# adaLN chunks of a two-layer diffusion backbone beside the first FFN: result columns on the tile's rows, products on GpSimd, row sums on ScalarE

## The chip, the cores and the metric

The kernel runs on one core of a Trainium2 chip. The metric is the device time of one execution in microseconds. A core has five engines that run side by side, each in its own program order: TensorE (PE; its weight loads are PEld), VectorE (DVE), ScalarE (ACT), GpSimd (POOL) and SyncE (SP), which here issues all DMAs. An engine waits at an instruction until the semaphores that it names are reached, and everything behind it on that engine waits too.

## What is computed

A batch of one: 512 latent tokens and 256 context tokens of width 1024 pass through two layers. Layer 0 mixes by windowed attention, layer 1 by a gated short convolution. Every layer takes six vectors of 1024 from the conditioning vector c (adaLN), which shift, scale and gate its two halves.

```
def adaln(cvec, w, b):
    m = (jax.nn.silu(cvec) @ w + b)[..., None, :]
    return jnp.split(m, 6, axis=-1)

for i in range(DEPTH):
    sh1, sc1, g1, sh2, sc2, g2 = adaln(c, ada_w[i], ada_b[i])
    ...
    h = h + g1 * y_lat
    h = h + g2 * conv_ffn(modulate(rms_norm(h, norm_ffn[i]), sh2, sc2), ffn_w_up[i], ffn_conv[i], ffn_w_down[i])

def conv_ffn(a, w_up, conv_w, w_down):
    g, u = jnp.split(dwconv3(a @ w_up, conv_w), 2, axis=-1)
    return (jax.nn.silu(g) * u) @ w_down
```

The hidden width of the FFN is 2816. A chunk of adaLN is one product of the vector silu(c) with a 1024x1024 matrix. All arrays are fp32.

## The kernel before

**Tiling.** Activations lie transposed: eight tiles of 128 channels by 512 tokens (`h`). A weight piece is a tile of 128x1024 that is loaded (`wraw`, four buffers), split by ScalarE into a high half (`whi`, a cast) and by VectorE into a low half (`wlo`, a subtraction), seven pieces in a ring (L177). Each product of a piece with an activation takes three matmuls, high by high, high by low and low by high (`mm3`, L195).

**FFN.** `ffn` (L808) goes through the hidden width in three thirds of 8, 8 and 6 tiles. For each hidden tile j two pieces of the up projection run over all eight channel tiles (48 matmuls of 512 columns); ScalarE and VectorE then evaluate the three taps of the convolution, silu and the product, and split the hidden tile into `g` tiles, high (ScalarE, L164) and low (VectorE, L165). After a third, `out_proj` (L759) runs its down projection, eight pieces, each over all hidden tiles of the third. The first four pieces of the first third run in two halves of 256 tokens, and the norm ahead of it is made in two halves as well (`norm_half`, L754): TensorE sums the squares over channels, ScalarE and VectorE take the root (`rcol`), TensorE spreads it over rows, and VectorE and ScalarE modulate eight tiles into `a`.

**adaLN.** The chunks that attention and the first norm need are made earlier. Seven chunks of 1024 results (the gate of the first FFN, and six for layer 1) are made beside the first FFN. `tail0` (L841) is called after each hidden tile with two steps and after each piece of the down projection with one. A step (`ada_step`, L239) takes 128 of the 1024 inputs: two loads of 128x512 into `araw` (four buffers); GpSimd multiplies each half by the column of silu(c) that belongs to its rows (L261) and adds it to an accumulator `adaacc` (L263). After eight steps, `ada_cols` (L277) turns the two accumulators with eight transposes on TensorE, VectorE sums each 128 columns (L274) and adds the bias (L275). The first of these GpSimd instructions waits for the end of the norm's second half (`add_manual_dep`, L253).

**Order.** In the attention an order written out by hand holds; from the FFN on, a scheduler orders each engine's instructions by its own estimate of when each can run, and that order is fixed in the program. Chip times do not change it.

Of the kernel before, what the change touches and what calls it, by code (L numbers as in the profile page):

```python
# [94 lines left out]
def kernel(ctx: ExitStack, tc: tile.TileContext, xT, ctxT, par_d, rope_d, mask_d, ident_d,  # L95
                         ada0_d, ada_d, wqkv_d, wo_d, wup_d, wdown_d, wsc_d, wsco_d, out_d):
    nc = tc.nc
    vec, act, pool, pe, sp = nc.vector, nc.scalar, nc.gpsimd, nc.tensor, nc.sync
# [8 lines left out]
    def nm(s):  # L107
        uid[0] += 1
        return f"{s}{uid[0]}"
# [15 lines left out]
    def nbank():  # L125
        t = ring[ringpos[0] % 8]
        ringpos[0] += 1
        return bank(t)
# [12 lines left out]
    ident = cp.tile([P, P], F32, name="ident")  # L141
# [94 lines left out]

    adastate = {}

    def ada_step(layer, ch, kt):  # L239

        raws = []
        for half in range(2):
            w = adastate["raw"]()
            sp.dma_start(out=w, in_=ada_d[layer, ch, kt, :, half * 512:(half + 1) * 512])
            raws.append(w)
        if kt == 0:
            adastate["acc"] = [adastate["acc_alloc"]() for _ in range(2)]
        acc = adastate["acc"]
        for half in range(2):
            ins = ada_mult_add(acc[half], raws[half], kt)  # L250
            after = adastate.pop("after", None)
            if after is not None:
                tc.add_manual_dep(ins.ins, after.ins.name, DEP, reason="the norm has VectorE's port for itself")  # L253
        if kt == KT - 1:
            adadone.append((layer, ch, acc))

    adadone = []

    def ada_mult_add(a, w, kt):
        c_ = cs[:, kt, 0:1]  # L260
        ins = pool.tensor_scalar(out=w if kt else a, in0=w, scalar1=c_, scalar2=1.0, op0=ALU.mult, op1=ALU.mult)  # L261
        if kt:
            pool.tensor_tensor(out=a, in0=a, in1=w, op=ALU.add)  # L263
        return ins

    def ada_transpose(acc, ps=None):
        ps = bank("qt") if ps is None else ps
        for i in range(4):
            pe.transpose(out=ps[:, i * P:(i + 1) * P], in_=acc[:, i * P:(i + 1) * P], identity=ident)
        return ps  # L270

    def ada_columns(layer, ch, half, ps):
        col = ada[layer][:, ch, half * 4:half * 4 + 4]
        vec.tensor_reduce(out=col, in_=ps.rearrange("p (a b) -> p a b", a=4), axis=AX.X, op=ALU.add)  # L274
        vec.tensor_tensor(out=col, in0=col, in1=pc("adab", (layer * 6 + ch) * KT + half * 4, 4), op=ALU.add)  # L275

    def ada_cols():  # L277

        layer, ch, acc = adadone.pop(0)
        banks = [ada_transpose(acc[half], nbank()) for half in range(2)]  # L280
        for half in range(2):
            ada_columns(layer, ch, half, banks[half])
# [11 lines left out]
    with ExitStack() as attn:  # L294
# [22 lines left out]
        with tc.tile_pool(name="start", bufs=1, reuse_waits="tile") as st:  # L317
# [10 lines left out]
            accs = {}  # L328
# [345 lines left out]
        def ad(i):  # L674
            for hf in range(2):
                tmps["a", i, hf] = w = ap.tile([P, 512], F32, tag="araw", name=nm("araw"), bufs=4)
                sp.dma_start(out=w, in_=ada_d[0, 2 + i // 8, i % 8, :, hf * 512:(hf + 1) * 512])

# [7 lines left out]
        def AT(ch, hf):  # L686
            tmps["A", ch, hf] = ada_transpose(accs[ch, hf])

        def AR(ch, hf):
            ada_columns(0, 2 + ch, hf, tmps["A", ch, hf])  # L690

# [11 lines left out]
    with tc.tile_pool(name="ffn", bufs=1, reuse_waits="tile") as fp, four_banks() as sp3:  # L703
# [3 lines left out]

        adastate["raw"] = lambda: fp.tile([P, 512], F32, tag="araw", name=nm("araw"), bufs=4)
        adastate["acc_alloc"] = lambda: fp.tile([P, 512], F32, tag="aacc", name=nm("adaacc"), bufs=4)

# [40 lines left out]
        def norm_begin(slot, shift):  # L751
            return {"acc": f(), "slot": slot, "shift": shift, "ah": [at() for _ in range(KT)], "al": [at() for _ in range(KT)]}
# [43 lines left out]
        lead_tail = [wpiece(None, 1024, raw) for raw in lead_raw]  # L796
        splits[:] = (3, 6)

        def last_cols():
            banks = [ada_transpose(accs[2, hf], nbank()) for hf in range(2)]  # L800
            for hf in range(2):
                ada_columns(0, 4, hf, banks[hf])
# [34 lines left out]

        late = [0, 0]
        fsteps = [(0, 5, kt) for kt in range(KT)] + [(1, ch, kt) for ch in (1, 0, 4, 3, 2, 5) for kt in range(KT)]
# [12 lines left out]

        def after_ffn0():
            assert not fsteps
            while adadone:
                ada_cols()
# [11 lines left out]
        first = proj([wpiece(wsc_d[i]) for i in (KT, 2 * KT, KT + 1, 2 * KT + 1)], ah, al, True, 4, second)  # L868
# [84 lines left out]
```

## Time and profile before

| what | us |
|---|---|
| median of three runs (lowest, highest) | 1238.05 (1236.66, 1239.66) |
| the profiled execution | 1238.28 |
| its span in the profile | 1236.5 |
| TensorE busy in the span | 1198.2 |
| VectorE, ScalarE, GpSimd busy | 733.0, 478.1, 401.7 |

The profile lists every instruction of one execution. A group row gives line, engine, operation, output and inputs with shapes and count; then the busy time in us and the mean of one in ns; then the idle time of the engine ahead of these instructions and what ended it. A timeline row gives the start and the duration in us, then the same names; in square brackets stands the idle time ahead of it. A row of waits names who waited, for whom, for how long in all, how often, and the longest. The time of an instruction includes what it loses once it has begun, for instance at a shared port. The first FFN runs on TensorE from about 290 to 688 us.

### The profile page before, as it was taken

The numbers are of one execution on the slowest core, as the hardware profiler recorded it, in microseconds if no ns is written. First come the engines' busy times: TensorE is split into PE (matmuls) and PEld (weight loads), VectorE is DVE, ScalarE is ACT, GpSimd is POOL, SyncE is SP. The second block draws the span as 40 slices with busy tenths as digits, with TensorE's granted clock in tenths as the row PEclk, the third lists the DMA queues.
The fourth block names the chain that finished last, engine by engine and source line by source line (L and its number), as shares of the span: only waits on it lengthen the run. The fifth ranks groups of instructions, "written<-read, shape, count | busy, mean of one in ns | idle before, by whom it ended". The sixth has DMA issues, their size and how long they took to land.

```text
span 1236.5 us, 16557 instructions
## 1 busy us (share of the span) xinstructions
PE 1198.2 (97%) x6414; PEld 980.2 (79%) x6414; DVE 733.0 (59%) x1128; ACT 478.1 (39%) x785; POOL 401.7 (32%) x358
## 2 busy tenths in 40 slices
PE   8999999999995999989999999999999999999998
PEld 6676666689883788878888988889988888888888
DVE  4688788647667545764665664444675446643652
ACT  4434777625334123322333442233454233432430
POOL 0059688510995893979601000001000000000000
PEclk8999999999997999999999999999999999999999
DMA  9445143252366455465423243332143233333211
GB/s 363 162 151 169 60 154 113 72 179 74 120 229 213 157 192 177 154 221 180 161 69 102 69 136 103 91 97 85 36 153 102 89 100 103 89 99 91 76 39 68
DMA packets 58382, 157.61 MB, mean 127 GB/s; under 512 B 6592, under 2 KB 8640, under 8 KB 58304
## 3 DMA queue, kind: packets, MB, share of 16 engines
q1 hardware_dynamic: 58304, 156.56, 38.6%
q8 instruction: 50, 0.82, 0.3%
q14 instruction: 28, 0.23, 0.1%
HBM read 152.86 MB, written 2.10 MB: 125 GB/s over the span
## 4 chain that ended last, share of the span: by engine, by line
PE 74%; POOL 12%; DVE 5%; issue 4%; DMA 2%; ACT 2%; SPq 0%; POOLq 0%; ACTq 0%; DVEq 0%
PE ps_s L198 10%; PE ps_s L196 10%; PE ps_s L197 10%; POOL adaacc L263 6%; PE ps_pt L196 5%; PE ps_pt L197 5%; PE ps_pt L198 5%; POOL araw L261 4%; PE ps_oa L660 3%; PE ps_pt L641 3%; PE ps_qt L197 2%; PE ps_qt L198 2%; PE ps_s L580 2%; PE ps_qt L196 2%; PE ps_oa L196 2%
## 5 line engine op out<-in xcount | busy, mean ns | idle before, releaser
L165 DVE TENSOR_TENSOR wlo<-wraw,whi 128x1024 fp32r<-128x1024 f32 (+2 forms) x194 | 228.0, 1183 | 183.9 <-ACT whi L164 179.0
L164 ACT CAST whi<-wraw 128x1024 fp32r<-128x1024 f32 (+2 forms) x194 | 183.3, 953 | 358.1 <-PE ps_s L197 153.0
L263 POOL TENSOR_TENSOR adaacc<-adaacc,araw 128x512 f32<-128x512 f32 x126 | 181.4, 1447 | 7.0
L196 PE MATMUL ps_s<-a,whi 128*128 128x512 f32 (+1 forms) x480 | 180.2, 375 | 0.0
L197 PE MATMUL ps_s<-a,whi 128*128 128x512 f32 (+1 forms) x480 | 180.1, 375 | 0.0
L198 PE MATMUL ps_s<-a,wlo 128*128 128x512 f32 (+1 forms) x480 | 179.9, 375 | 0.0
L261 POOL TENSOR_SCALAR araw<-araw,cs 128x512 f32<-128x512 f32 x140 | 128.1, 918 | 39.0 <-DMA araw<-in_ada 39.0
L196 PE MATMUL ps_s<-g,whi 128*128 128x512 f32 (+1 forms) x304 | 105.2, 346 | 17.3 <-ACT g L164 17.3
L197 PE MATMUL ps_s<-g,whi 128*128 128x512 f32 (+1 forms) x304 | 104.6, 345 | 0.0
L198 PE MATMUL ps_s<-g,wlo 128*128 128x512 f32 (+1 forms) x304 | 104.4, 344 | 0.0
L196 PEld LDWEIGHTS ps_s<-a,whi 128*128 128x128 f32 x480 | 90.4, 188 | 16.2
L198 PEld LDWEIGHTS ps_s<-a,wlo 128*128 128x128 f32 x480 | 90.4, 188 | 16.2
L197 PEld LDWEIGHTS ps_s<-a,whi 128*128 128x128 f32 x480 | 90.4, 188 | 16.1
L198 PE MATMUL ps_pt<-a,wlo 128*128 128x512 f32 (+1 forms) x256 | 92.9, 363 | 0.0
L196 PE MATMUL ps_pt<-a,whi 128*128 128x512 f32 (+1 forms) x256 | 92.9, 363 | 0.0
L197 PE MATMUL ps_pt<-a,whi 128*128 128x512 f32 (+1 forms) x256 | 92.8, 362 | 0.0
L749 DVE SCALAR_TENSOR_TENSOR h<-ps_s,ada,h 128x512 f32<-128x512 f32 (+1 forms) x45 | 28.3, 631 | 88.0 <-PE ps_s L198 87.9
L164 ACT CAST g<-f 128x512 fp32r<-128x512 f32 x52 | 32.3, 621 | 123.2 <-DVE f L826 122.6
L196 PEld LDWEIGHTS ps_s<-g,whi 128*128 128x128 f32 x304 | 57.7, 190 | 25.8 <-ACT g L164 18.4
L207 POOL TENSOR_TENSOR f<-f,t 128x512 f32<-128x512 f32 x6 | 9.5, 1582 | 205.0 <-ACT t L206 205.0
L197 PEld LDWEIGHTS ps_s<-g,whi 128*128 128x128 f32 x304 | 57.7, 190 | 8.2 <-DVE g L165 0.8
L198 PEld LDWEIGHTS ps_s<-g,wlo 128*128 128x128 f32 x304 | 57.8, 190 | 7.1
(297 smaller groups left out, 2518.6 us busy)
## 6 DMA issues: line engine op xcount, KB each, us to landing
wraw<-in_wup SPq DMA_DIRECT2D x88, 512.0 KB, 3.6
araw<-in_ada SPq DMA_DIRECT2D x160, 256.0 KB, 2.7
wraw<-in_wdown SPq DMA_DIRECT2D x32, 512.0 KB, 3.7
wraw<-in_wsc SPq DMA_DIRECT2D x24, 512.0 KB, 3.5
gw<-in_ada SPq DMA_DIRECT2D x16, 512.0 KB, 10.0
wraw<-in_wqkv SPq DMA_DIRECT2D x12, 512.0 KB, 7.1
wraw<-in_wdown SPq DMA_DIRECT2D x16, 384.0 KB, 3.1
wraw<-in_wo SPq DMA_DIRECT2D x8, 512.0 KB, 5.2
```

The source lines that it names most:

```text
L164: act.copy(out=hi, in_=raw)
L165: vec.tensor_tensor(out=lo, in0=raw, in1=hi.bitcast(F32), op=ALU.subtract)
L196: pe.matmul(out=ps, lhsT=wh, rhs=ah, start=start, stop=False)
L197: pe.matmul(out=ps, lhsT=wh, rhs=al, start=False, stop=False)
L198: pe.matmul(out=ps, lhsT=wl, rhs=ah, start=False, stop=stop)
L207: eng.tensor_tensor(out=acc, in0=acc, in1=sq[:, :n], op=ALU.add)
L261: ins = pool.tensor_scalar(out=w if kt else a, in0=w, scalar1=c_, scalar2=1.0, op0=ALU.mult, op1=ALU.mult)
L263: pool.tensor_tensor(out=a, in0=a, in1=w, op=ALU.add)
L580: pe.matmul(out=s[t][:, i, :w], lhsT=q2s[p][x][HALF[t], cl], rhs=KEYS[p // 4][(p // 2 + t) % 2][y][HALF[t], ks_], start=(n == 0), stop=(n ...
L641: pe.transpose(out=pt[:, q:q + P], in_=es[p, b, t][0][:, o:o + P], identity=ident)
L660: pe.matmul(out=r["po"][HALF[t], b0:b0 + n], lhsT=V[:, j, p // 2, :], rhs=pf[:, t * n:(t + 1) * n], start=first, stop=not r["left"])
L749: vec.scalar_tensor_tensor(out=h[m][:, cl], in0=ps[:, cl], scalar=gate[:, m:m + 1], in1=h[m][:, cl], op0=ALU.mult, op1=ALU.add)
```

## The change

The same seven chunks are made from another layout. The host stores these weights transposed (`adat`), so that a tile of 128x1024 has 128 result columns on its rows and the 1024 inputs along the row. Once, after the last columns of the earlier chunks, TensorE transposes the eight columns of silu(c), each spread over 128 columns, and ScalarE copies the result into `crow`, a tile that holds silu(c) in every row. A step is then one load of 512 KB (`araw`, three buffers), one GpSimd product of the tile with `crow` (in place), and one ScalarE copy whose accumulator gives the 128 row sums, which go straight to the column of `ada`. The bias is added by VectorE once a chunk. Accumulators, transposes and column sums of these chunks go. Before a new tile is asked for, `tail0` issues the sums of all but the last tile in hand. The wait for the norm is now put on the first tile's product alone.

```diff
+        adaq = [(0, 5, m) for m in range(KT)] + [(1, ch, m) for ch in (1, 0, 4, 3, 2, 5) for m in range(KT)]
+
+        def ada_tile(after=None):
+
+            layer, ch, m = adaq.pop(0)
+            w = fp.tile([P, 1024], F32, tag="araw", name=nm("araw"), bufs=3)
+            sp.dma_start(out=w, in_=adat_d[6 * layer + ch - 5, m])
+            ins = pool.tensor_tensor(out=w, in0=w, in1=crow, op=ALU.mult)
+            if after is not None:
+                tc.add_manual_dep(ins.ins, after.ins.name, DEP, reason="the norm has VectorE's port for itself")
+            adaps.append((layer, ch, m, w))
+
+        def ada_sum():
+            layer, ch, m, w = adaps.pop(0)
+            col = ada[layer][:, ch, :]
+            act.activation(out=w, in_=w, func=AF.Copy, accum_out=col[:, m:m + 1])
+            if m == KT - 1:
+                vec.tensor_tensor(out=col, in0=col, in1=pc("adab", (layer * 6 + ch) * KT, KT), op=ALU.add)
...
+        crow = fp.tile([P, 1024], F32, name="crow")
         def last_cols():
...
+            for half in range(2):
+                ps = nbank()
+                for i in range(4):
+                    pe.transpose(out=ps[:, i * P:(i + 1) * P], in_=cs[:, half * 4 + i, 0:1].broadcast_to([P, P]), identity=ident)
+                act.copy(out=crow[:, half * 512:(half + 1) * 512], in_=ps)
...
         def tail0(n):
-            late.append(len(adadone))
-            if late[-3] and adadone:
-                ada_cols()
-                late[-2:] = [v - 1 for v in late[-2:]]
-            if "first" not in adastate:
-                adastate["first"] = adastate["after"] = nf["end"]
             for _ in range(n):
-                if fsteps:
-                    ada_step(*fsteps.pop(0))
+                while len(adaps) > 1 or adaps and not adaq:
+                    ada_sum()
+                if adaq:
+                    ada_tile(nf["end"] if held else None)
+                    held.clear()
```

The scheduler places the new instructions as follows. First GpSimd, about the norm ahead of the first FFN: L207 adds up the norm's squares, and the numbered names are single buffers. Before, two scalings stand ahead of it and the rest behind the first `adaacc`, which is the instruction that waits for the norm's end:

```order
L261 TENSOR_SCALAR araw_3647<-araw_3647,cs 128x512
L261 TENSOR_SCALAR araw_3649<-araw_3649,cs 128x512
L207 TENSOR_TENSOR f_2929<-f_2929,t_3049 128x512
L207 TENSOR_TENSOR f_2929<-f_2929,t_3053 128x512
L261 TENSOR_SCALAR adaacc_3643<-araw_3639,cs 128x512
L261 TENSOR_SCALAR adaacc_3644<-araw_3641,cs 128x512
L263 TENSOR_TENSOR adaacc_3643<-adaacc_3643,araw_3647 128x512
```

The same place of GpSimd in the changed kernel, where `araw_3652` is the first tile, the one whose product waits for the norm's end:

```order
L207 TENSOR_TENSOR f_2930<-f_2930,t_3054 128x512
L684 TENSOR_TENSOR araw_3655<-araw_3655,crow 128x1024
L684 TENSOR_TENSOR araw_3739<-araw_3739,crow 128x1024
L684 TENSOR_TENSOR araw_3743<-araw_3743,crow 128x1024
L684 TENSOR_TENSOR araw_3827<-araw_3827,crow 128x1024
L684 TENSOR_TENSOR araw_3831<-araw_3831,crow 128x1024
L684 TENSOR_TENSOR araw_3913<-araw_3913,crow 128x1024
L684 TENSOR_TENSOR araw_3917<-araw_3917,crow 128x1024
L684 TENSOR_TENSOR araw_3997<-araw_3997,crow 128x1024
L684 TENSOR_TENSOR araw_4002<-araw_4002,crow 128x1024
L684 TENSOR_TENSOR araw_4082<-araw_4082,crow 128x1024
L684 TENSOR_TENSOR araw_4086<-araw_4086,crow 128x1024
```

Then follow `araw_4166` and only then `araw_3652`: twelve products now stand ahead of the one that waits, where before all accumulation stood behind the wait.

Second ScalarE, at the start of the norm's first half: L206 squares a half tile of `h`, L221 takes the root, L164 splits a weight. Before:

```order
L206 ACTIVATE t_3104<-h_2905 128x256
L206 ACTIVATE t_3132<-h_2907 128x256
L206 ACTIVATE t_3160<-h_2909 128x256
L206 ACTIVATE t_3188<-h_2911 128x256
L164 CAST whi_3366<-wraw_3364 128x512 x2
L206 ACTIVATE t_3216<-h_2905 128x256
L164 CAST whi_3657<-wraw_3655 128x512
L221 ACT_TABLE_LOAD
L221 ACTIVATE rcol_3250<-ps_s_3247,epst 128x2
```

And in the changed kernel, where L694 is a row sum:

```order
L694 ACTIVATE araw_3655,ada_73<-araw_3655 128x1024
L694 ACTIVATE araw_3739,ada_73<-araw_3739 128x1024
L206 ACTIVATE t_3117<-h_2905 128x256
L206 ACTIVATE t_3145<-h_2907 128x256
L206 ACTIVATE t_3173<-h_2909 128x256
L694 ACTIVATE araw_3743,ada_73<-araw_3743 128x1024
L206 ACTIVATE t_3201<-h_2911 128x256
L694 ACTIVATE araw_3827,ada_73<-araw_3827 128x1024
L206 ACTIVATE t_3229<-h_2905 128x256
L164 CAST whi_3379<-wraw_3377 128x512 x2
L694 ACTIVATE araw_3831,ada_73<-araw_3831 128x1024
L221 ACT_TABLE_LOAD
```

Five sums have come in ahead of the norm's first root; nine stand ahead of the second root, and fifteen ahead of the first convolution tap of the FFN.

Third ScalarE at the end of the first third's up projection: L725 is a convolution tap, L818 silu, `g_4161` the high half of the third's last hidden tile. Before (L738, L825, `g_4197`):

```order
L738 ACTIVATE f_4187<-ps_oa_4131,par 128x512
L825 ACTIVATE f_4187<-f_4187 128x512
L164 CAST whi_4487<-wraw_4485 128x1024
L738 ACTIVATE f_4191<-ps_pt_4162,par 128x512
L164 CAST g_4197<-f_4187 128x512
```

And in the changed kernel:

```order
L694 ACTIVATE araw_4965,ada_74<-araw_4965 128x1024
L818 ACTIVATE f_4151<-f_4151 128x512
L694 ACTIVATE araw_5045,ada_74<-araw_5045 128x1024
L164 CAST whi_4392<-wraw_4390 128x1024
L725 ACTIVATE f_4155<-ps_qt_4126,par 128x512
L694 ACTIVATE araw_5049,ada_74<-araw_5049 128x1024
L694 ACTIVATE araw_5129,ada_74<-araw_5129 128x1024
L164 CAST g_4161<-f_4151 128x512
```

Of the 56 sums, 37 stand ahead of `g_4161`; the other 19 stand among the nine weights that follow, and the last one ahead of the first tap of the second third.

More of the change, by code (lines that the diff above doesn't have):

```diff
@@ L95 @@
 def kernel(ctx: ExitStack, tc: tile.TileContext, xT, ctxT, par_d, rope_d, mask_d, ident_d,
-                         ada0_d, ada_d, wqkv_d, wo_d, wup_d, wdown_d, wsc_d, wsco_d, out_d):
+                         ada0_d, ada_d, adat_d, wqkv_d, wo_d, wup_d, wdown_d, wsc_d, wsco_d, out_d):
     nc = tc.nc
@@ L235, in modulate, with ada_transpose @@
         return vec.scalar_tensor_tensor(out=lo, in0=n, scalar=sh, in1=hi.bitcast(F32), op0=ALU.add, op1=ALU.subtract)
[L237 to L257, printed above, removed]
     def ada_mult_add(a, w, kt):
         c_ = cs[:, kt, 0:1]
-        ins = pool.tensor_scalar(out=w if kt else a, in0=w, scalar1=c_, scalar2=1.0, op0=ALU.mult, op1=ALU.mult)
+        pool.tensor_scalar(out=w if kt else a, in0=w, scalar1=c_, scalar2=1.0, op0=ALU.mult, op1=ALU.mult)
         if kt:
             pool.tensor_tensor(out=a, in0=a, in1=w, op=ALU.add)
-        return ins
-    def ada_transpose(acc, ps=None):
-        ps = bank("qt") if ps is None else ps
+    def ada_transpose(acc, ps):
         for i in range(4):
@@ L270, in ada_transpose, with ada_columns @@
         return ps
-    def ada_columns(layer, ch, half, ps):
-        col = ada[layer][:, ch, half * 4:half * 4 + 4]
+    def ada_columns(ch, half, ps):
+        col = ada[0][:, ch, half * 4:half * 4 + 4]
         vec.tensor_reduce(out=col, in_=ps.rearrange("p (a b) -> p a b", a=4), axis=AX.X, op=ALU.add)
[L275 to L282, printed above, removed]
+        vec.tensor_tensor(out=col, in0=col, in1=pc("adab", ch * KT + half * 4, 4), op=ALU.add)
     def scale_cols(dst, sc, gain):
@@ L676, in ad @@
                 tmps["a", i, hf] = w = ap.tile([P, 512], F32, tag="araw", name=nm("araw"), bufs=4)
-                sp.dma_start(out=w, in_=ada_d[0, 2 + i // 8, i % 8, :, hf * 512:(hf + 1) * 512])
+                sp.dma_start(out=w, in_=ada_d[i // 8, i % 8, :, hf * 512:(hf + 1) * 512])
         def ap_(i, hf):
@@ L686, in AT @@
         def AT(ch, hf):
-            tmps["A", ch, hf] = ada_transpose(accs[ch, hf])
+            tmps["A", ch, hf] = ada_transpose(accs[ch, hf], bank("qt"))
         def AR(ch, hf):
-            ada_columns(0, 2 + ch, hf, tmps["A", ch, hf])
+            ada_columns(2 + ch, hf, tmps["A", ch, hf])
         steps = dict(kv=kv_, kt=kt_, qr=qr_, T=T_, V=V_, c=c_, ap=ap_, wr=wr, wh=wh, wl=wl, ks=ks, kd=kd, vc=vc, kr=kr, ka=ka, kz=kz, kn=kn,
@@ L706 @@
         wcount[0] = 4
-        adastate["raw"] = lambda: fp.tile([P, 512], F32, tag="araw", name=nm("araw"), bufs=4)
-        adastate["acc_alloc"] = lambda: fp.tile([P, 512], F32, tag="aacc", name=nm("adaacc"), bufs=4)
+        adaq = [(0, 5, m) for m in range(KT)] + [(1, ch, m) for ch in (1, 0, 4, 3, 2, 5) for m in range(KT)]
[7 more added lines that the diff above has]
+            adaps.append((layer, ch, m, w))
+        adaps = []
+        def ada_sum():
[4 more added lines that the diff above has]
+                vec.tensor_tensor(out=col, in0=col, in1=pc("adab", (layer * 6 + ch) * KT, KT), op=ALU.add)
         def f(dt=F32):
@@ L836, in ffn @@
             return nx
-        late = [0, 0]
-        fsteps = [(0, 5, kt) for kt in range(KT)] + [(1, ch, kt) for ch in (1, 0, 4, 3, 2, 5) for kt in range(KT)]
+        held = [True]
         def tail0(n):
-            late.append(len(adadone))
-            if late[-3] and adadone:
-                ada_cols()
-                late[-2:] = [v - 1 for v in late[-2:]]
-            if "first" not in adastate:
-                adastate["first"] = adastate["after"] = nf["end"]
-            for _ in range(n):
-                if fsteps:
-                    ada_step(*fsteps.pop(0))
+            for _ in range(n):
+                while len(adaps) > 1 or adaps and not adaq:
[3 more added lines that the diff above has]
+                    held.clear()
         def after_ffn0():
-            assert not fsteps
-            while adadone:
-                ada_cols()
+            assert not adaq
+            while adaps:
+                ada_sum()
             scale_cols(smod[:, 3, :], ada[1][:, 1, :], pc("gmix", 8, 8))
@@ L931 @@
     arrays["ada0"] = np.ascontiguousarray(a0.transpose(4, 0, 2, 1, 3, 5)).reshape(KT, 2, P, 1024)
-    arrays["ada"] = np.ascontiguousarray(aw.transpose(0, 3, 1, 2, 4))
+    arrays["ada"] = np.ascontiguousarray(aw[0, :, :, 2:5].transpose(2, 0, 1, 3))
+    at = inp["ada_w"].reshape(2, D, 6, KT, P).transpose(0, 2, 3, 4, 1)
+    arrays["adat"] = np.ascontiguousarray(at.reshape(12, KT, P, D)[5:])
     wq = inp["win_w_qkv"][0].reshape(4, 2, P, 3, 512)
@@ L947 @@
         kernel(tc, args["xT"], args["ctxT"], args["par"], args["rope"], args["mask"], args["ident"],
-                             args["ada0"], args["ada"], args["wqkv"], args["wo"], args["wup"], args["wdown"],
+                             args["ada0"], args["ada"], args["adat"], args["wqkv"], args["wo"], args["wup"], args["wdown"],
                              args["wsc"], args["wsco"], out)
```

2 lines of the change are left out of this document (1 added, 1 removed).

## The prediction

> **What bounds the kernel now.** I read the page's busy line first, then the waits of TensorE in the stretch of the first FFN, then TensorE's timeline there.
>
> ```profile
> span 1236.5 us, 16557 instructions
> ...
> PE 1198.2 (97%) x6414; PEld 980.2 (79%) x6414; DVE 733.0 (59%) x1128; ACT 478.1 (39%) x785; POOL 401.7 (32%) x358
> PE ps_s L196 <- ACT g L164: 17.3, 2, 8.8
> PE ps_pt L196 <- ACT g L164: 3.4, 1, 3.4
> 392.95 0.79 PE L196 MATMUL ps_s<-g,whi 128*128 128x512 f32 x1 [8.76 <-ACT g L164]
> 403.82 0.80 PE L196 MATMUL ps_s<-g,whi 128*128 128x512 f32 x1 [8.49 <-ACT g L164]
> 543.36 0.70 PE L196 MATMUL ps_pt<-g,whi 128*128 128x512 f32 x1 [3.36 <-ACT g L164]
> ```
>
> TensorE is the bound. Its waits between 245 and 640 us are these three, 20.7 us in all, each where a down projection begins and ScalarE has not yet made the hidden tile g that the projection ends with. So the change is judged by when ScalarE finishes the last g of the first third. Call that moment X: now 403.8 us. The next rows say why it is so late.
>
> ```profile
> SPq L244 <- POOL adaacc L263: 177.4, 92, 4.0
> 308.01 31.20 SPq L244 DMA_DIRECT2D araw<-in_ada  x15
> 339.31 0.37 SPq L172 DMA_DIRECT2D wraw<-in_wup  x1
> 343.10 1.05 ACT L164 CAST whi<-wraw 128x1024 fp32r<-128x1024 f32 x1 [15.19 <-DMA wraw<-in_wup]
> L263 POOL TENSOR_TENSOR adaacc<-adaacc,araw 128x512 f32<-128x512 f32 x98 | 145.4, 1492 | 4.7
> L261 POOL TENSOR_SCALAR araw<-araw,cs 128x512 f32<-128x512 f32 x96 | 95.2, 996 | 26.0 <-DMA araw<-in_ada 26.0
> 307.29 1.36 POOL L261 TENSOR_SCALAR adaacc<-araw,cs 128x512 f32<-128x512 f32 x2 [37.91 <-issue]
> ```
>
> Fifteen adaLN loads stand in SyncE's queue ahead of a weight tile, each waiting for a buffer that GpSimd frees; ScalarE idles 15.2 us for that weight, and from there ScalarE and VectorE run behind TensorE until X. GpSimd is busy from 307.29 (before that it waits for the norm to end) with instructions that are longer than they need be. The next rows show what makes them so.
>
> ```profile
> 319.42 1.13 POOL L261 TENSOR_SCALAR araw<-araw,cs 128x512 f32<-128x512 f32 x1
> 320.64 1.77 POOL L263 TENSOR_TENSOR adaacc<-adaacc,araw 128x512 f32<-128x512 f32 x1
> 318.95 1.04 DVE L826 TENSOR_TENSOR f<-f,f 128x512 f32<-128x512 f32 x1
> 321.17 1.78 DVE L165 TENSOR_TENSOR g<-f,g 128x512 fp32r<-128x512 f32 x1
> L165 DVE TENSOR_TENSOR wlo<-wraw,whi 128x1024 fp32r<-128x1024 f32 x51 | 62.5, 1225 | 58.9 <-ACT whi L164 57.3
> L165 DVE TENSOR_TENSOR g<-f,g 128x512 fp32r<-128x512 f32 x22 | 15.2, 692 | 13.6 <-ACT g L164 13.6
> L165 DVE TENSOR_TENSOR wlo<-wraw,whi 128x1024 fp32r<-128x1024 f32 x49 | 74.9, 1528 | 54.3 <-ACT whi L164 53.0
> ```
>
> VectorE's g starts at 321.17, while GpSimd's add of 320.64 runs until 322.41; it ends at 322.95, which is 0.54 us later, about its own 0.69 (the second FFN's row, where GpSimd is idle). Two-input VectorE instructions on SBUF and GpSimd's instructions **take turns**; each waits for the other's whole instruction. The split wlo costs 1.225 us in the second FFN (x51) and 1.528 beside GpSimd (x49).
>
> At this place the Trainium skill, "SBUF — State Buffer", in the section on the doors to SBUF, speaks against the change: it calls the port pair of VectorE and GpSimd an exclusive lock, held for a whole instruction, not a share of bandwidth. The four timed rows agree. By that rule a product twice as long makes VectorE wait longer each time, and the sum below comes out at X near 419; if instead the mean surcharge of the rows (0.30 us for a wlo) stayed as it is, X would be 400 or less.
>
> **The change part by part.** Rows for the prices:
>
> ```profile
> L482 POOL TENSOR_TENSOR e<-t x4: 738/740/747, 67.1 to 81.0; 128x256 f32<-128x256 f32 x4
> L263 POOL TENSOR_TENSOR adaacc<-adaacc,araw x126: 1262/1293/2377, 79.8 to 604.5; 128x512 f32<-128x512 f32 x126
> L164 ACT CAST whi<-wraw 128x1024 fp32r<-128x1024 f32 x142 | 148.8, 1050 | 312.0 <-PE ps_s L197 134.6 <-issue 46.8 <-PE ps_pt L197 46.4
> L595 ACT ACTIVATION_READ_ACCUMULATOR e<-e,nmx 128x1 f32 x64 | 12.3, 192 | 0.0
> L625 ACT COPY R<-ps_qt 128x512 f32<-128x512 f32 x8 | 4.7, 584 | 4.0 <-PE ps_qt L621 4.0
> 267.32 1.15 ACT L206 ACTIVATE t<-h 128x512 f32<-128x512 f32 x2
> 265.55 0.60 PE L269 MATMUL ps_oa<-ident,g 128*128 128x128 f32 x4
> 265.99 0.60 PE L269 MATMUL ps_pt<-ident,g 128*128 128x128 f32 x4
> wraw<-in_wup SPq DMA_DIRECT2D x88, 512.0 KB, 3.6
> 340.88 1.36 POOL L261 TENSOR_SCALAR adaacc<-araw,cs 128x512 f32<-128x512 f32 x2
> 385.18 1.36 POOL L261 TENSOR_SCALAR adaacc<-araw,cs 128x512 f32<-128x512 f32 x2
> ```
>
> *GpSimd.* Removed for seven chunks: 112 scalings and 98 adds. The two grouped rows above hold 98 adds and 96 scalings in 240.6 us, some 192 without the turns (98 x 1.29 + 96 x 0.68, by the x2 at 307.29). Added: 56 products of 128x1024. From 256 to 512 columns the price rises from 0.74 to 1.29, so 1024 columns cost 1.29 + 1.10 = 2.39 us, 134 us in all. The bounds are 1.97 (the second half at a scaling's pace, 1.29 + 0.68) and 2.58 (2 x 1.29); I take 2.39, which two rows of the same form give.
>
> *ScalarE.* Added: 56 sums, each like a 1024-wide cast plus the accumulator's read: 1.05 + 0.19 = 1.24 us (1.05 if the read hides), 69 us in all, and two copies of 0.58 for silu(c). ScalarE has idle time for them, but it runs in order: behind each sum that waits for its product stand a weight's cast, a conv's tap or a hidden tile.
>
> *TensorE.* Removed: 56 transposes of 0.11 us (four from 265.55 to 265.99), 6.2 us. A chunk's first scaling starts at 307.29, 340.88 and 385.18, so two chunks are through before X and the transposes of five, 40, fall behind it: 4.4 us off the path. Eight new ones (0.9 us) fall before X and cost nothing while TensorE waits there; without that cover, 0.9 us.
>
> *SyncE and VectorE.* 56 loads of 512 KB (3.6 us to landing, like a weight's) instead of 112 of 256 KB: as many bytes, so nothing by itself. Fourteen short reductions and fourteen adds of four columns go, seven adds come: under 10 us of VectorE beside other work, at nothing.
>
> *The wait on the norm* holds back the first product only. By the new order GpSimd computes twelve others ahead of it, and eleven sums stand on ScalarE ahead of the last two modulates of the norm's second half. So products run through the norm, where the port had been VectorE's. What the norm takes there now:
>
> ```profile
> 285.48 0.26 ACT L221 ACTIVATE rcol<-ps_s,epst 128x2 f32<-128x2 f32 x1
> 298.98 0.26 ACT L221 ACTIVATE rcol<-ps_s,epst 128x2 f32<-128x2 f32 x1 [4.25 <-PE ps_s L215]
> 306.25 0.88 DVE L235 SCALAR_TENSOR_TENSOR a<-t,ada,a 128x256 fp32r<-128x256 f32 x2 [0.18 <-ACT a L234]
> L235 DVE SCALAR_TENSOR_TENSOR a<-t,ada,a 128x256 fp32r<-128x256 f32 x48 | 21.8, 479 | 1.3 <-ACT a L234 1.3
> L207 DVE TENSOR_TENSOR f<-f,t 128x256 f32<-128x256 f32 x24 | 10.1, 422 | 5.4 <-ACT t L206 5.3
> 270.64 1.22 DVE L165 TENSOR_TENSOR wlo<-wraw,whi 128x1024 fp32r<-128x1024 f32 x1
> 271.77 0.42 DVE L207 TENSOR_TENSOR f<-f,t 128x256 f32<-128x256 f32 x1
> ```
>
> Five sums stand ahead of the first rcol and nine ahead of the second. With one buffer held by the product that waits, two go round: sum 1.24, load 3.6, product 2.39, so two products in 7.2 us at best. Walking ScalarE's new order with that from 269.6 us puts the first rcol near 295 (285.5 now), the second near 313 (299.0) and the norm's end near 328 (307.1). TensorE comes to the down projection at 392.95 - 8.76 = 384 now, and then some 17 us later (the norm's 21 less what it has in hand), near 401. That is still before X, so it is not added; from 18 us more it would be.
>
> *X* by the shared port: products can begin when silu(c) is spread, at 267.32 + 1.15 + 2 x 0.58 = 269.6. By ScalarE's order, 37 of the 56 sums stand ahead of the last g of the first third; now two chunks of eight steps and part of the third are done by then (the rows of 340.88 and 385.18). Their products: 37 x 2.39 = 88.4 us. VectorE's own instructions on the port up to there, counted in its order: 17 full wlo (20.8), 28 instructions of 512 columns (19.4), 32 of the norm (15.3), nine adds (4.1): 59.6 us, less 0.09 for each of the 86, since one starts before the last has ended (271.77 against 270.64 + 1.22): 51.9. Together X is at least 269.6 + 88.4 + 51.9 = 409.9. The port also stands idle: after the 15th sum ScalarE issues 17 others, some 12 us, while three buffers give GpSimd only 7.2 us of work. In the norm, the two buffers' turns of 7.2 us leave gaps too. I take 9 us (0 to 17): **X = 419**.
>
> *The sum.* X moves by 419 - 403.8 = +15.2. At the second boundary 19 products are left to spread over nine weights, and behind them no GpSimd work: the wait of 3.4 us goes; what is late next there is TensorE itself. Transposes: -4.4. Net +7.4 us. The profiled execution took 1238.3 us (span 1236.5 and 1.8 around it), the median of the runs is 1238.05; so I forecast **1245.7 us**.
>
> **Rivals.**
> *As meant (faster).* The loads no longer hold up weights, and neither g is waited for: -17.3 - 3.4 - 6.2 + 0.9 = -26, **1212**. For it: 134 us of GpSimd work instead of more than 192. Against it: 37 sums in order ahead of X. It needs the port and the sums to be through when TensorE arrives at 384, and the ledger exceeds that by 26. Chance 0.08.
> *Turns cheaper than the ledger (faster).* If a product takes 1.97 us (37 x 0.42 = 15.5 less) or VectorE finds the gaps between products at the present surcharge, X is near 400: -3.8 - 3.4 - 4.4 = -11.6, **1227**. It decides for faster as soon as X is below 409, and for slower X must pass 414. For it: VectorE's port work is an upper count, since conv and residual leave it gaps to fall into. Against it: the rows at 321.17. Chance 0.20.
> *Loads decide (much slower).* If each turn of three buffers also waits for ScalarE's work in order (three casts, 3.2), it takes 1.24 + 3.6 + 2.39 + 3.2 = 10.4 us, a tile 3.5, and the last 22 of the 37, which the walk begins near 355, end at 432: +28.2 - 7.8 = +20.4, **1259**. For it: SyncE puts weights that wait for VectorE ahead of adaLN loads. Chance 0.20.
> *The forecast's case:* X from 409 to 427. Chance 0.52, of which 0.10 lies within 0.2% (2.5 us, about what a measurement of this kernel can tell from no change).
>
> **How the numbers follow.** Faster 0.08 + 0.20 = 0.28; within 0.2% 0.10; slower 0.42 + 0.20 = 0.62. The range leaves out the first rival and the tail of the third: 1222 to 1262. The forecast's own range is 1236 to 1254.
>
> **What would show it.** Right: products from about 270 us on, before the norm's end; VectorE's norm instructions far above 0.48 us; the norm's end 10 to 25 us later; ScalarE's sums with idle time put down to GpSimd; TensorE's wait for the last g of the first third up to some 419; no wait at the second boundary. Wrong: that wait gone, or products much under 2.39 us; or new waits of TensorE for weights in the down projection or the second third, which I put at none because seven split pieces lie ahead.

## The result, and the profile after

| what | before | after |
|---|---|---|
| median of four runs each (lowest, highest), us | 1238.35 (1236.66, 1239.66) | 1253.0 (1250.55, 1254.82) |
| span of the profiled execution, us | 1236.5 | 1251.2 |
| ratio after / before, 95% interval | | 1.0118 (1.0096 to 1.0139) |

The changed kernel is 1.2% slower, 14.7 us. First the page's span and busy line of the changed kernel, then the two largest of TensorE's waits between 245 and 660 us (us in total, times, longest), then the rows of its timeline in which it waits at the first down projection.

```profile
span 1251.2 us, 16317 instructions
...
PE 1196.5 (96%) x6366; PEld 978.2 (78%) x6366; DVE 744.7 (60%) x1107; ACT 540.3 (43%) x899; POOL 302.1 (24%) x204
PE ps_s L196 <- ACT g L164: 22.2, 2, 14.9
PE ps_pt L225 <- DVE rcol L222: 5.2, 1, 5.2
414.05 0.80 PE L196 MATMUL ps_s<-g,whi 128*128 128x512 f32 x1 [14.88 <-ACT g L164]
418.05 0.79 PE L197 MATMUL ps_s<-g,whi 128*128 128x512 f32 x1 [3.21 <-DVE g L165]
427.48 0.79 PE L196 MATMUL ps_s<-g,whi 128*128 128x512 f32 x1 [7.36 <-ACT g L164]
```

GpSimd is busy for 302.1 us instead of 401.7, yet TensorE waits longer for the last hidden tiles of the first third. X, the last of these moments, is 427.5 us (403.8 before). The wait at the second boundary (3.36 us before) is gone. TensorE reaches the first wait at 414.05 - 14.88 = 399.2.

Next the groups of the products and the sums over the whole span (busy and mean of one, then idle time ahead of them), and two groups of VectorE between 262 and 430 us, with the last norm instruction ahead of the FFN.

```profile
L684 POOL TENSOR_TENSOR araw<-araw,crow 128x1024 f32<-128x1024 f32 x56 | 150.0, 2700 | 62.6 <-DMA araw<-in_adat 59.7 <-DVE a L235 2.6
L694 ACT ACTIVATE araw<-araw 128x1024 f32<-128x1024 f32 x56 | 59.2, 1057 | 60.7 <-POOL araw L684 60.4
L165 DVE TENSOR_TENSOR wlo<-wraw,whi 128x1024 fp32r<-128x1024 f32 x18 | 34.0, 1900 | 8.6 <-ACT whi L164 8.6
L235 DVE SCALAR_TENSOR_TENSOR a<-t,ada,a 128x256 fp32r<-128x256 f32 x16 | 16.1, 1009 | 0.7 <-ACT a L234 0.7
325.69 0.48 DVE L235 SCALAR_TENSOR_TENSOR a<-t,ada,a 128x256 fp32r<-128x256 f32 x1 [0.18 <-ACT a L234]
```

A product takes 2.70 us on the mean, with what it loses at the port. The norm's instructions cost VectorE 1.01 us each (0.48 alone), a weight's low half 1.90 (1.23 alone). The norm ends at 326.2 (307.1 before). The idle numbers show the waits: GpSimd 59.7 us for loads (26.0 for its scalings before), and ScalarE, newly, 60.4 us for products. How they hang together shows in one stretch, on GpSimd, ScalarE and SyncE in turn (start, duration, what waited).

```profile
335.98 4.78 POOL L684 TENSOR_TENSOR araw<-araw,crow 128x1024 f32<-128x1024 f32 x2 [0.15 <-DMA araw<-in_adat]
350.69 4.39 POOL L684 TENSOR_TENSOR araw<-araw,crow 128x1024 f32<-128x1024 f32 x1 [9.93 <-DMA araw<-in_adat]
358.98 2.58 POOL L684 TENSOR_TENSOR araw<-araw,crow 128x1024 f32<-128x1024 f32 x1 [3.90 <-DMA araw<-in_adat]
372.15 10.92 POOL L684 TENSOR_TENSOR araw<-araw,crow 128x1024 f32<-128x1024 f32 x4 [10.60 <-DMA araw<-in_adat]
344.82 0.63 ACT L818 ACTIVATE f<-f 128x512 f32<-128x512 f32 x1
345.35 1.04 ACT L694 ACTIVATE araw<-araw 128x1024 f32<-128x1024 f32 x1
346.96 1.04 ACT L694 ACTIVATE araw<-araw 128x1024 f32<-128x1024 f32 x1
346.51 0.33 SPq L683 DMA_DIRECT2D araw<-in_adat  x1
347.53 5.65 SPq L172 DMA_DIRECT2D wraw<-in_wup  x4
353.23 0.42 SPq L683 DMA_DIRECT2D araw<-in_adat  x1
359.32 4.89 SPq L172 DMA_DIRECT2D wraw<-in_wdown  x3
364.26 0.90 SPq L683 DMA_DIRECT2D araw<-in_adat  x2
```

The gap of 9.93 us ahead of 350.69: GpSimd is through at 340.76, but the sum that frees a buffer stands on ScalarE behind other work and starts only at 345.35, 4.6 us after that (and 9.5 us after its own product, the last of four that GpSimd ended at 335.8); its load goes out at 346.51 and arrives 4 us later. The next gap: a buffer is free from 348.0, but four weights stand ahead in SyncE's queue, and the load goes out at 353.23. Before the gap of 10.60, three weights go out from 359.32 to 364.2 and two loads behind them. The three buffers are used in turn, and the first of these two loads fills the one that is free from 349.1, when the next sum (348.00) ends; so it stands 15 us behind weights and one load, and then takes 7.8 us to arrive. So both queues hold the loads back, ScalarE's with the sums and SyncE's with weights, and the load itself takes 4 to 8 us here.

### The profile page after: what moved, and what is told of

Same layout as the page of the kernel before. It is cut to its first block, busy times and chain, and to the rows that moved or that the text cites. A ratio compares the mean times of both kernels' runs of the same rounds, so it can differ in the third digit from the quotient of the medians.

```text
span 1251.2 us, 16317 instructions
## 1 busy us (share of the span) xinstructions
PE 1196.5 (96%) x6366; PEld 978.2 (78%) x6366; DVE 744.7 (60%) x1107; ACT 540.3 (43%) x899; POOL 302.1 (24%) x204
## 4 chain that ended last, share of the span: by engine, by line
PE 78%; DVE 7%; issue 4%; POOL 4%; ACT 3%; DMA 3%; SPq 0%; POOLq 0%; DVEq 0%; ACTq 0%
PE ps_s L197 11%; PE ps_s L198 11%; PE ps_s L196 11%; PE ps_pt L196 5%; PE ps_pt L198 5%; PE ps_pt L197 5%; PE ps_oa L629 3%; PE ps_pt L610 3%; PE ps_oa L196 3%; PE ps_oa L197 3%; PE ps_oa L198 3%; PE ps_qt L198 3%; PE ps_qt L197 3%; PE ps_qt L196 3%; DMA araw<-in_adat 3%
## 5 line engine op out<-in xcount | busy, mean ns | idle before, releaser
L164 ACT CAST whi<-wraw 128x1024 fp32r<-128x1024 f32 (+2 forms) x194 | 183.1, 952 | 284.5 <-PE ps_s L197 124.2
L197 PE MATMUL ps_s<-a,whi 128*128 128x512 f32 (+1 forms) x480 | 176.7, 368 | 0.0
L198 PE MATMUL ps_s<-a,wlo 128*128 128x512 f32 (+1 forms) x480 | 176.5, 368 | 0.0
L196 PE MATMUL ps_s<-a,whi 128*128 128x512 f32 (+1 forms) x480 | 176.5, 368 | 0.0
L684 POOL TENSOR_TENSOR araw<-araw,crow 128x1024 f32<-128x1024 f32 x56 | 150.0, 2700 | 62.6 <-DMA araw<-in_adat 59.7
L196 PE MATMUL ps_s<-g,whi 128*128 128x512 f32 (+1 forms) x296 | 107.1, 362 | 22.2 <-ACT g L164 22.2
L197 PE MATMUL ps_s<-g,whi 128*128 128x512 f32 (+1 forms) x296 | 106.6, 361 | 3.7 <-DVE g L165 3.7
L197 PE MATMUL ps_pt<-a,whi 128*128 128x512 f32 (+1 forms) x256 | 94.8, 370 | 2.5 <-DVE a L235 2.5
L207 POOL TENSOR_TENSOR f<-f,t 128x512 f32<-128x512 f32 x6 | 9.5, 1580 | 359.1 <-ACT t L206 359.1
L196 PE MATMUL ps_pt<-a,whi 128*128 128x512 f32 (+1 forms) x256 | 94.7, 370 | 0.7 <-ACT a L234 0.7
L694 ACT ACTIVATE araw<-araw 128x1024 f32<-128x1024 f32 x56 | 59.2, 1057 | 60.7 <-POOL araw L684 60.4
L164 ACT CAST g<-f 128x512 fp32r<-128x512 f32 x52 | 32.2, 620 | 99.5 <-DVE f L819 98.9
```

Source lines behind the costliest of these rows:

```text
L164: act.copy(out=hi, in_=raw)
L196: pe.matmul(out=ps, lhsT=wh, rhs=ah, start=start, stop=False)
L197: pe.matmul(out=ps, lhsT=wh, rhs=al, start=False, stop=False)
L198: pe.matmul(out=ps, lhsT=wl, rhs=ah, start=False, stop=stop)
L207: eng.tensor_tensor(out=acc, in0=acc, in1=sq[:, :n], op=ALU.add)
L684: ins = pool.tensor_tensor(out=w, in0=w, in1=crow, op=ALU.mult)
```

## The experiments

Twelve kernels ran, each beside the kernel before. X below is the moment of TensorE's last wait for a hidden tile of the first third.

| kernel | median, us | ratio to before, 95% interval | X, us |
|---|---|---|---|
| changed kernel | 1253.0 | 1.0118 (1.0096 to 1.0139) | 427.5 |
| without products | 1215.1 | 0.9804 (0.9776 to 0.9832) | 392.4 |
| without sums | 1258.7 (one run) | | 434.3 |
| without loads | 1233.0 (the profiled execution; a second one took 4136) | | 409.6 |
| all products behind the norm | 1244.3 | 1.0041 (1.0021 to 1.0061) | 409.2 |
| loads in ScalarE's queue | 1242.5 | 1.0038 (1.0023 to 1.0054) | 411.7 |
| paced | 1257.4 | 1.0147 (1.0127 to 1.0167) | 403.0 |
| sums behind the cast | 1233.8 | 0.9965 (0.9951 to 0.9979) | 393.6 |
| lagged (that, and paced) | 1227.0 | 0.9916 (0.9899 to 0.9933) | 394.6 |
| paced, ScalarE's queue | 1237.1 | 0.9994 (0.9979 to 1.0008) | 394.3 |
| sums behind the cast, ScalarE's queue | 1220.0 | 0.9851 (0.9829 to 0.9874) | 388.5 |
| lagged, ScalarE's queue | 1210.7 | 0.9777 (0.976 to 0.9794) | no wait |
| the kernel before, paced | 1246.7 | 1.006 (1.0042 to 1.0078) | 393.9 |

### One part taken out at a time

Without products:

```diff
-            ins = pool.tensor_tensor(out=w, in0=w, in1=crow, op=ALU.mult)
...
```

> Leaves out the 56 products (the sums read the loaded rows unscaled); loads, sums and their places in ScalarE's order stay, with 46 sums instead of 37 ahead of the last hidden tile of the first third. Theory (the products' turns on the shared port are most of the lateness): VectorE's norm instructions cost 0.48 us and wlo 1.23 us again, X 388 to 405, time 1216 to 1232. Rival (loads behind weights in SyncE's queue decide): ScalarE's sums wait for loads as GpSimd did, X 415 or later, time 1240 or more. Rival (the sums' own 1.24 us on ScalarE decide, 46 of them 57 us): ScalarE busy without gaps up to X, X 410 or later.

TensorE's wait at the first down projection:

```profile
392.42 0.49 PE L196 MATMUL ps_s<-g,whi 128*128 128x512 f32 x1 [2.80 <-ACT g L164]
```

The theory held, with the time 0.9 us below its range: without the products TensorE waits only 2.8 us here, though all 56 loads and 56 sums stay and 46 sums stand ahead of X. Without products there is no loss.

Without sums:

```diff
-            act.activation(out=w, in_=w, func=AF.Copy, accum_out=col[:, m:m + 1])
+            act.activation(out=col[:, m:m + 1], in_=w[:, 0:1], func=AF.Copy)
```

> Leaves out the row sums: in their place ScalarE copies one column of each product, with the same waits. Loads and products stay; 42 instead of 37 of them stand ahead of the last hidden tile of the first third. Theory (the sums cost by their place in ScalarE's order, behind products, and hardly by their 1.24 us): X 415 or later, time 1240 or more. Rival (the sums' own time on ScalarE, 37 x 1.24 = 46 us, decides): X at 395 or less, time 1225 or less.

```profile
434.30 0.79 PE L196 MATMUL ps_s<-g,whi 128*128 128x512 f32 x1 [10.30 <-ACT g L164]
```

The theory held. X is even later; 42 short copies, each waiting for its product, stand ahead of it instead of 37 sums, which goes with that but isn't tested by itself. What the sums cost is their place behind a product, not their 1.24 us.

Without loads:

```diff
-            sp.dma_start(out=w, in_=adat_d[6 * layer + ch - 5, m])
-            ins = pool.tensor_tensor(out=w, in0=w, in1=crow, op=ALU.mult)
+            ins = pool.tensor_tensor(out=w, in0=crow, in1=crow, op=ALU.mult)
```

> Leaves out the 56 loads of adaLN rows (each product multiplies the spread silu(c) by itself); products, sums and buffers stay, with 40 sums instead of 37 ahead of the last hidden tile of the first third. Theory (turns of the port, with loads adding the idle time beyond the ledger): X = 269 + 40 x 2.49 + 52 of VectorE = 420 less what overlaps, with almost no idle port: 408 to 418, time 1233 to 1244, some 10 to 19 us under the changed kernel. Rival (port turns alone, loads were hidden): X 424 to 430, time within 3 us of 1253. Rival (loads alone decide): X at TensorE's own arrival, 400 or less, time 1225 or less.

GpSimd's first stretch of products, and X:

```profile
306.81 14.86 POOL L683 TENSOR_TENSOR araw<-crow 128x1024 f32<-128x1024 f32 x8 [38.65 <-DVE a L235]
409.59 1.22 PE L196 MATMUL ps_s<-g,whi 128*128 128x512 f32 x2 [8.46 <-ACT g L164]
```

X and the time lie where the theory put them, but for reasons that it had only in part. The scheduler now put the product that waits for the norm first, so nothing ran in the norm; and a product of a tile with itself is cheaper, 1.86 us (14.86 / 8). It does show that with loads gone X still comes 17 us after the 392.4 of the kernel without products, so loads alone do not decide. The profile is of the execution of 1233.0; why the other took 4136 us is open.

All products behind the norm:

```diff
-                    ada_tile(nf["end"] if held else None)
-                    held.clear()
+                    ada_tile(nf["end"])
```

> Every product waits for the end of the norm, as all of GpSimd's adaLN work did before the change; nothing else differs but the order that follows from it: 4 sums instead of 15 stand on ScalarE ahead of the first conv tap's hidden tile, 27 instead of 37 ahead of the last hidden tile of the first third. Theory (port turns plus sums in order): the norm ends near 307 again instead of 326, its VectorE instructions cost 0.48 us again, but 27 products then stand behind it: 307 + 27 x 2.49 = 374 plus VectorE's port work behind the norm, some 34 us, and some 9 us of idle port: X 408 to 418, time 1236 to 1246, a few us under the changed kernel. Rival (the norm's lateness of 19 us goes straight through to X): X 408 or less, time 1234 or less. Rival (loads behind weights decide): X stays at 425 to 432, time within 3 us of the changed kernel's 1253.

VectorE's norm instructions (262 to 430 us) and X:

```profile
L235 DVE SCALAR_TENSOR_TENSOR a<-t,ada,a 128x256 fp32r<-128x256 f32 x16 | 7.2, 478 | 0.4 <-ACT a L234 0.4
409.17 0.79 PE L196 MATMUL ps_s<-g,whi 128*128 128x512 f32 x1 [11.89 <-ACT g L164]
```

As the theory had it: the norm is itself again, and 27 products behind it still hold X at 409. X comes 18 us earlier than in the changed kernel, but the time falls by only 8.7; a wait of 7.48 us for a hidden tile of the second third, at 551.56, which the changed kernel doesn't have, takes most of the rest back.

### The loads' queue

```diff
-            sp.dma_start(out=w, in_=adat_d[6 * layer + ch - 5, m])
+            act.dma_start(out=w, in_=adat_d[6 * layer + ch - 5, m])
```

> Only the adaLN loads move, from SyncE's queue to ScalarE's, so that no weight stands ahead of them; with that the order of the sums shifts to 25 instead of 37 ahead of the last hidden tile of the first third (12 instead of 15 ahead of the first conv tap). Theory (GpSimd's idle time is loads held behind weights): GpSimd waits for loads for under 25 us instead of 56 between 262 and 430 us, X 390 to 408, time 1218 to 1233. Rival (three buffers set the pace, whatever the queue): GpSimd waits for loads 40 us or more, X 415 or later, time 1241 or more.

GpSimd's wait for loads between 262 and 430 us, then a sum on ScalarE and the load into the buffer that it frees:

```profile
POOL araw L684 <- DMA araw<-in_adat: 51.3, 17, 9.8
331.92 1.06 ACT L694 ACTIVATE araw<-araw 128x1024 f32<-128x1024 f32 x1 [0.39 <-POOL araw L684]
343.05 0.40 ACTq L683 DMA_DIRECT2D araw<-in_adat  x1
```

The theory fell. GpSimd waits for loads nearly as long as before (55.7 us), and the time is that of the rival (X lies between the two). A load behind weights in SyncE's queue has become a load behind ScalarE's own work: the buffer is free at 333.0, the load goes out at 343.05. The kernel is 10.5 us faster, with 25 sums ahead of X instead of 37; which of the two did it isn't told apart.

### The order

Paced: each product waits for the newest hidden tile's low part (or residual).

```diff
-                    split(cv[0], hi, lo)
+                    pace[0] = split(cv[0], hi, lo)
...
-                    ada_tile(nf["end"] if held else None)
-                    held.clear()
+                    ada_tile(pace[0])
```

> Each product waits for the newest hidden tile's or residual's VectorE instruction, so that products and sums are spread two to a hidden tile: 12 sums instead of 37 stand on ScalarE ahead of the last hidden tile of the first third, and none ahead of the first. Theory (how many products stand ahead of X decides, each at its turn of the port and in ScalarE's order): the norm ends near 307, X comes to where TensorE arrives, 384 to 392, and no later boundary waits more than some 5 us; time 1212 to 1225, faster than both kernels. Rival (each product has its price wherever it stands, since the port's turns just move to later hidden tiles): what is gained before X is lost at the second boundary or inside the second third; time 1238 or more. Rival (loads decide): they now wait for paced buffers in SyncE's queue ahead of weights, and TensorE waits for weights L164/L165 for more than 10 us in all; time 1235 to 1250.

The theory fell by 32 us at least; the time of the first rival (1238 or more) came, but for another reason. One hidden tile on ScalarE, with the two products beside it, and VectorE in the second one:

```profile
375.91 0.62 ACT L164 CAST g<-f 128x512 fp32r<-128x512 f32 x1 [2.88 <-DVE f L821]
377.34 5.74 POOL L684 TENSOR_TENSOR araw<-araw,crow 128x1024 f32<-128x1024 f32 x2 [7.53 <-DVE g L165]
379.76 1.07 ACT L694 ACTIVATE araw<-araw 128x1024 f32<-128x1024 f32 x1 [1.69 <-POOL araw L684]
383.11 1.06 ACT L694 ACTIVATE araw<-araw 128x1024 f32<-128x1024 f32 x1 [2.19 <-POOL araw L684]
384.16 0.61 ACT L820 ACTIVATE f<-f 128x512 f32<-128x512 f32 x1
389.18 0.62 ACT L164 CAST g<-f 128x512 fp32r<-128x512 f32 x1 [2.88 <-DVE f L821]
385.75 1.23 DVE L165 TENSOR_TENSOR wlo<-wraw,whi 128x1024 fp32r<-128x1024 f32 x1 [3.49 <-ACT whi L164]
377.52 3.29 DVE L165 TENSOR_TENSOR wlo<-wraw,whi 128x1024 fp32r<-128x1024 f32 x1 [0.26 <-ACT whi L164]
380.73 0.74 DVE L726 SCALAR_TENSOR_TENSOR f<-ps_oa,par,f 128x511 f32<-128x511 f32 x1
```

From one cast of g to the next it is 13.27 us: low part, two products, two sums, silu, and the next cast. The two sums stand ahead of the next tile's silu, so the pacing closed a loop. Some 5 us of it pass between silu (384.16) and cast (389.18): there VectorE waits for a weight's high half, makes its low half (the row of 385.75), then two taps and the product with silu's result. TensorE's 48 matmuls of a tile start some 0.227 us apart and take 10.9 (the casts are 10.88 us apart in the second third of the kernel without products), not the 11.3 of the expectations. VectorE's low half of a weight waits for a whole product (3.29 us), while the convolution, which reads one input from PSUM, runs beside one at its own 0.74.

Sums behind the cast: each sum waits on ScalarE for the next hidden tile's cast; products stay free.

```diff
+                    cast[0], _ = split(cv[0], hi, lo)
...
+            while adaps:
+                ada_sum(cast[0])
             for _ in range(n):
-                while len(adaps) > 1 or adaps and not adaq:
-                    ada_sum()
```

> Only the place of the sums changes: each waits for the next hidden tile's cast on ScalarE, as in the lagged kernel, but the products are free again (the first waits for the norm, the others for load and buffer, as in the changed kernel). Again 10 sums ahead of the last hidden tile of the first third. Theory (what costs is sums in ScalarE's order ahead of the hidden tiles; three buffers then pace the products by themselves): like the lagged kernel, time 1222 to 1232, X 390 to 398. Rival (products that start when they like take the port at the wrong moments, so their pacing mattered): 1238 or more.

Lagged: the same, and each product paced as above.

> As in the paced kernel each product waits for the newest hidden tile's low part on VectorE, but each sum now stands on ScalarE behind the next hidden tile's cast, one tile later: 10 sums ahead of the last hidden tile of the first third. Theory (the paced kernel ran in a loop of 13.2 us a hidden tile, low part, two products, two sums, silu, cast, low part, against 11.3 us of TensorE work; the loop is now cut): ScalarE's wait for products is below 5 us in all, TensorE's waits for g are below 5 us at each boundary, X 385 to 394, time 1212 to 1226. Rival (turns of the port: wlo takes 3.3 us beside a product and VectorE cannot keep 11.3 us a tile): the waits for g stay at some 10 us a boundary, time 1240 or more.

TensorE's wait at the first down projection with the sums behind the cast, then its waits at the first two boundaries of the lagged kernel:

```profile
393.57 0.80 PE L195 MATMUL ps_s<-g,whi 128*128 128x512 f32 x1 [7.43 <-ACT g L164]
394.62 0.79 PE L195 MATMUL ps_s<-g,whi 128*128 128x512 f32 x1 [8.05 <-ACT g L164]
533.78 0.79 PE L195 MATMUL ps_s<-g,whi 128*128 128x512 f32 x1 [5.40 <-ACT g L164]
```

The sums' place alone takes 19.2 us off the changed kernel; X is as expected, the time 1.8 us above the range. Pacing the products, with the order that follows from it, takes 6.8 more. The lagged kernel just misses its ranges: the time is 1.0 us above, X 0.6, and the waits for g are 8.05 and 5.40 us, not below 5.

### Order and queue together

> The place of the sums and ScalarE's queue for the adaLN loads together, products free. Theory: as the lagged kernel with ScalarE's queue, no wait for g over 2 us at any boundary, time 1207 to 1215. Rival (free products on the port cost): 1220 or more.

> The lagged kernel with the adaLN loads issued from ScalarE's queue, behind the sum that frees their buffer, instead of SyncE's. Theory (with the products spread out, loads hold up nothing): within 4 us of the lagged kernel. Rival (in SyncE's queue the loads wait for buffers ahead of weights and hold these up): faster than the lagged kernel by more than 4 us, with fewer ScalarE waits for wraw.

> The first paced kernel (sums ahead of the next silu) with the adaLN loads in ScalarE's queue. Theory (the loop low part, two products, two sums, silu, cast sets 13.2 us a hidden tile, whatever queue loads use): TensorE waits some 10 us for g at each boundary, time 1243 or more. Rival (loads in SyncE's queue made the paced kernel slow): time 1225 or less.

The lagged kernel with ScalarE's queue, its busy line and all of TensorE's waits for hidden tiles from 245 to 660 us:

```profile
PE 1190.0 (98%) x6366; PEld 974.6 (81%) x6366; DVE 746.1 (62%) x1107; ACT 538.7 (45%) x899; POOL 294.9 (24%) x204
PE ps_oa L195 <- ACT g L164: 1.7, 1, 1.7
```

This version beats both kernels: 1210.7 us, 0.9777 of the time before. With free products it is 9.3 us slower (1220.0), and TensorE waits 4.1, 2.4 and 2.0 us at the boundaries. The theory of no wait over 2 us and 1207 to 1215 fell, and the time is at the edge of the rival, that products that start when they like do cost; this agrees with the 6.8 us above. With the other queue each of four orders gained: 10.5 us (changed), 20.3 (paced), 13.8 (sums behind the cast), 16.3 (lagged). The theories that gave the queue nothing in the lagged kernel, and left the paced one at 1243 or more, fell; so did the rival that the queue was all. The paced kernel with ScalarE's queue still waits 9.5, 8.0 and 4.9 us at the boundaries, but its casts are 12.06 us apart instead of 13.27 in most of the second third, so the loop had no fixed length. It isn't settled what share is the queue's: with it the scheduler also put other instructions elsewhere. In the lagged kernel ScalarE now runs some of the convolutions' first taps ahead of a silu or of two sums, where they had run behind these.

The kernel before, paced in the same way:

```diff
-            if "first" not in adastate:
-                adastate["first"] = adastate["after"] = nf["end"]
...
+                    adastate["after"] = pace[0]
                     ada_step(*fsteps.pop(0))
```

> The kernel before, with each adaLN step (two scalings and two adds on GpSimd) waiting for the newest hidden tile's or residual's VectorE instruction, and no sums on ScalarE. Theory (the order around the hidden tiles was the cost before as well; the change's layout is not needed for the gain): X 386 to 396, second boundary's wait below 4 us, time 1218 to 1230. Rival (four short instructions a step are too much port time for 11.3 us a hidden tile: two steps of 4 us and VectorE's 3.7): X 400 or later and waits at the second boundary, time 1235 or more.

```profile
393.85 0.80 PE L196 MATMUL ps_s<-g,whi 128*128 128x512 f32 x1 [8.89 <-ACT g L164]
PE ps_pt L269 <- POOL adaacc L263: 15.6, 1, 15.6
```

X falls by 10 us, but the old chunks are not done when the first FFN ends: TensorE waits 15.6 us for the last one's transposes. So this pacing alone gains nothing in the old layout. Both theory and rival missed where the time would go.

## Why the prediction was right, and what it sized wrong

*What bounds the kernel* held: the wait for the last hidden tiles of the first third decides. X moved by 427.5 - 403.8 = +23.7 us, where +15.2 was forecast; less the wait of 3.4 at the second boundary, which went as forecast, and 4.4 of transposes, that gives +15.9, and the span grew by 14.7. (From X to the end it is 823.7 us instead of 832.7, 9.0 less, where the two terms make 7.8.) So the direction came by the forecast path, and the size was twice the +7.4 of the forecast.

*The walk through the norm* held: its roots were put near 295 and 313 and came at 292.1 and 312.6, its end near 328 and came at 326.2, TensorE's arrival near 401 and came at 399.2. That the products run in the norm, by the order, was read rightly; holding them all behind the norm gave 8.7 us back.

*The port's ledger* held in its work and not in its gaps. Laid on one axis from the first product at 268.7 to X at 427.5, GpSimd's products and VectorE's instructions with two inputs in SBUF cover 137.3 us (a union of the timeline's rows). Forecast were 88.4 + 51.9 = 140.3. The port has none of them under way for the other 21.5 us. **The step that was mis-sized is "I take 9 us (0 to 17)" of idle port**: 269.6 + 140.3 + 9 = 419 against 268.7 + 137.3 + 21.5 = 427.5, half a microsecond beyond the forecast's own case of 409 to 427. The rows from 335.98 on show what fills it in its longest gaps: sums late in ScalarE's order, the load's own 4 to 8 us, and weights ahead of loads in SyncE's queue. The prediction had the first (17 instructions of some 12 us behind the 15th sum), but put the third only into the rival "loads decide", at X = 432; the measurement lies between the two, nearer to the rival. That rival's mechanism is in part true: the rows show weights ahead of loads, while the run with the loads in ScalarE's queue shows that taking the weights away leaves GpSimd's wait at 51.3 us.

*"As meant"* was given 1212, on the condition that port and sums are through when TensorE arrives. The order that meets that condition, lagged with ScalarE's queue, took 1210.7. So the gain that the prediction worked out was there, in another order and another queue; 37 sums in order ahead of X, each behind its product, stood in front of it. How much of it the layout gives is not shown: the kernel before, whose loads stood ahead of weights in SyncE's queue, did not run with its loads in ScalarE's. *"Turns cheaper"* fell: a product took 2.70 us on the mean, waits included, and 2.34 at the least, not 1.97, and a weight's low half paid 0.67 us more (1.90 against 1.23), not 0.30.

The cause of the slower time, by the runs: load, product and sum form a chain, and the sums stand in it ahead of the hidden tiles on ScalarE. The loss goes when any one link does: without products (1215.1), without loads (1233.0, with cheaper products and another order), or with the sums in another place (1233.8, 19.2 us back). It doesn't go with the sums' duration (1258.7 without). What the chain is made of is shown; how the last 16 us of the queue split between queue and order stays open, and so does what more than three buffers would do, since no run has them.

## What to carry to other kernels

An engine that runs in order turns an instruction with slack into a wait for everything behind it. Before work is moved to such an engine, ask what stands behind it there, and place it behind the latency-bound chain of the same round, with its input ready a round earlier. A dependency that paces work must not be released by an instruction that itself stands behind that work: count the loop's length against the bound's period.

## What the runs showed of the hardware that was not expected

A wait of TensorE costs more than its length. TensorE's rows in the changed kernel after the wait of 7.36 us, then the stretch from 399 to 428 us and the six us after it in the table by windows (window, length, busy of PE, PEld, DVE, ACT and POOL, granted clock, DMA share, GB/s):

```profile
428.07 0.63 PE L198 MATMUL ps_s<-g,wlo 128*128 128x512 f32 x1
428.50 0.63 PE L196 MATMUL ps_s<-g,whi 128*128 128x512 f32 x1
...
433.87 0.40 PE L196 MATMUL ps_s<-g,whi 128*128 128x512 f32 x1
434.10 0.40 PE L197 MATMUL ps_s<-g,whi 128*128 128x512 f32 x1
399.00:428.00 29.00, 3.55 (x7) 1.95 (x7) 24.70 (x18) 15.92 (x28) 23.43 (x9) 0.57 0.61 207
428.00:434.00 6.00, 5.53 (x14) 3.82 (x13) 3.80 (x3) 3.34 (x5) 5.34 (x3) 0.53 0.63 230
```

For some six us after the wait the matmuls start 0.43 us apart instead of 0.23, at a granted clock of 0.53; then the pace is whole again. That is 14 matmuls in a stretch that has room for 26, a loss of some 2.7 us (6.0 - 14 x 0.235), of which 0.47 is a further short wait. The pace was already half ahead of this wait: after the one of 14.88 us the few matmuls from 418.64 on start 0.43 us apart too. How long it stays so differs: 6.1 us from the first matmul here, 3.2 in the kernel before (the wait of 8.49 us at 403.82), 3.8 in the lagged kernel (8.05 us at 394.62). A shorter wait can do it as well: after the 2.80 us in the kernel without products the matmuls start 0.43 us apart from 393.3 to 396.3. The Trainium skill, "TensorE: Matmul & The Clock Gate", section "What's actually happening", says that the clock is halved after an idle window of about 3.4 us and comes back after one busy window of that length; the trace agrees with the halving, but the return took from 3.2 to 6.1 us, and a wait of 2.80 us was enough.

Moving loads to another queue gained 10 to 20 us in four orders. The Trainium skill, "DMA: Bandwidth & Descriptors", section "Issuing engines are not separate DMA queues", says that this saves only the time to issue a DMA, usually a small one. For bandwidth no run here shows otherwise; but what stands in which queue, and the order that a scheduler makes of it, were worth more than issue time.
